# A hybrid decoder layer on one core: the first FFN matrix's operands behind the last load of w_out, the second gate product between the token groups, low halves one unit ahead

## The chip, the core and the metric

The kernel runs on one core of one Trainium2 chip. PE is its matrix engine (its weight loads are listed as PEld), DVE the vector engine, ACT the scalar engine, POOL a general engine, SP the engine that issues most DMAs. Each engine takes its instructions strictly in the order of the program and waits on semaphores for the others. The metric is the device time of one execution in microseconds.

## What is computed

One inference step of one decoder layer, for a prompt of 1024 tokens and for 8 samples of one token each, with d_model 1024 and d_ff 2816. All data is fp32. Cut to its core:

```python
def layer(x, c):
    sh, sc, gt = split(silu(c) @ w_ada_mix + b_ada_mix, 3)
    h = x * (1 + sc) + sh
    q, k, v, rq, rk, rv, rg = split(h @ w_in)
    att = window_attention(rope(q), rope(k), v, sinks)      # 8 heads of 64, window 128
    ret = silu(rg) * group_norm(retention(rope(rq), rope(rk), rv))  # 4 heads of 128, chunks of 128
    x = layer_norm(ALPHA * x + (1 + gt) * (concat(att, ret) @ w_out))
    sh, sc, gt = split(silu(c) @ w_ada_ffn + b_ada_ffn, 3)
    g, u = split((x * (1 + sc) + sh) @ w_up, 2)
    return layer_norm(ALPHA * x + (1 + gt) * ((silu(g) * u) @ w_down))
```

The samples use cached keys, values and retention states instead of earlier tokens, and the new keys, values and states are outputs too.

## The kernel before, in words

**Products.** An fp32 product is made from three reduced-precision ones. Every operand x is split into a high half (a cast, on ACT, line 269 for weights and 1347 for others) and a low half, x minus the high half (a subtraction on DVE, line 281 for weights, 1348 for others). `mm3` (line 213) then issues high×high, high×low and low×high (lines 215, 216, 217 of the profile). So no product on line 216 with a weight's low half (`wl`) can run before DVE has made it.

**Weight pages.** The input and output projections take their weights in units of one page (128 x 1024). `w_get` returns unit i and sets others on their way by `depth` = [loads, high halves, low halves] ahead of it. At first it is [2, 1, 0]. In the second half of the output projection it is set to [4, 4, 3].

**Stages.** After the start come the input projections of two halves of 512 tokens, then the output projection of half 0 and of half 1 (`out_proj`, line 1128). Each half runs over two column groups (cg) of 512 columns, four units of w_out each (kp), and four tiles of 128 tokens (t). The w_out units are the pages 46 to 53 for half 0 and 54 to 61 for half 1. All four tiles are computed per unit, except for the last column group of half 1, pages 58 to 61 (`by_tile`): there tile 0 goes through all units first, then tiles 1, 2 and 3, each followed by its own output and layer norm. The samples' share of the output projection (`poutz`) rides along in half 1. Then come layer norm 1 (`ln1_tile`, and `ln1_s` for the samples), the modulated, transposed FFN input of a token group of 512 tokens (`h2_group`: transposes into `h2p` on PE, `ht` on ACT, the differences `ts` and the halves `hb`, `hs`, `hc` on DVE and ACT), 22 up matrices and the down pass, and layer norm 2.

**The FFN.** Two by two blocks of a product are made with seven products instead of eight, so sums of blocks of the weights are needed besides the blocks. `up_prep(n)` releases all steps due up to n: the loads of a matrix (`wr`), its four sums on DVE (`sa`, `sb`, lines 1366 to 1369), and its halves `wa`, `wb`, `wc`, `wd`. For the first matrix, `out_proj` calls it between the last tiles (t == 1: loads, t == 2: sums and the first halves). `f_end` makes such sums from a finished pair of FFN tiles (`fsa`, `fsb`), and `wd_sums` from w_down (`wta`, `wtb`).

**The order of the work.** Main generators (projections, FFN) hand out costs in ns. The class `Merge` interleaves side generators with them: attention, retention, sample work, gate products, norms. A generator that yields "need" waits until that name is in `done`; other yields give the PE cost and how long to pause. A scheduler then orders the instructions of DVE, ACT and POOL by its own estimates, so what finally stands in a row on an engine is told by the built program, not by the code alone.

**Other parts that the change touches.** `ada_gate_a` and `ada_gate_b` make the gate of a sublayer: eight loads of 512 KB (`adr`), four blocks of products (`adab`, line 878), and two selections (`gsels`, line 902). Number 1 gates the mixer, number 2 the FFN. Both run before the output projection of half 0 or in it. `samp_ret` updates the samples' retention states with 32 DVE operations (line 994) from pages `st` and `vb`. `samp_sum` adds the four row groups in which PE leaves the samples' products. `ret_M` scales the retention output and splits it. In the last product of the down pass (`finish`) the first KM of its 11 units are computed for four tiles together, and the rest tile by tile in an order written by hand, each tile followed by its norm. A page pool of 46 pages and a pool of 8 PSUM banks hold everything.

## Time and profile before

| | us |
|---|---|
| median of 3 runs | 1256.14 |
| lowest, highest | 1255.63, 1257.42 |
| the profiled run | 1258.56 |
| its span | 1256.8 |

The mean granted clock of PE in the profiled run was 0.980. A row of the profile's timeline gives start, length, engine, line, operation, output and inputs by the program's names, shapes and, in brackets, how long the engine stood idle before and what released it. Records that follow one another closely are joined (x4), and the lengths of PE's matmuls overlap, since they are pipelined; from one start to the next is the pitch.

### The profile page before, as it was taken

To read this page: it belongs to the slowest core of one execution; us is meant where nothing else is said; L and a number is where in the kernel's file an instruction comes from. 1 tells how busy PE (TensorE), PEld (TensorE's weight loads), DVE (VectorE), ACT (ScalarE), POOL (GpSimd) and SP (SyncE) were. 2 spreads that over 40 slices of the span, in tenths; PEclk is the share of its full clock that TensorE was granted. 3 is DMA by queue.
4 is the path that set the end of the run, shared out by engine and by line. 5 is a ranking of instruction groups with operands and counts; after the bars stand their busy time and mean duration, and the time that the engine had idled before them with its cause. 6 is when DMAs were issued, how large, how long until landed. Compare 5 with 4: busy or idle time off the path is not lost.

```text
span 1256.8 us, 20184 instructions
## 1 busy us (share of the span) xinstructions
PE 1213.2 (97%) x7923; PEld 1023.8 (81%) x7923; DVE 875.0 (70%) x1749; ACT 469.6 (37%) x876; POOL 93.9 (7%) x130
## 2 busy tenths in 40 slices
PE   8999989999999999987999999999999999999996
PEld 5877756788877677677999999999999987888885
DVE  3456665787654687877767676667666769849697
ACT  2345543355543335545232322232223234434420
POOL 0000000001000002020110111011101110000011
PEclk8999999999999999997999999999999999999998
DMA  9732387242226432412443444344434499746631
GB/s 290 230 118 68 125 271 258 68 153 87 68 68 217 147 124 79 149 69 68 147 165 109 163 156 159 110 156 156 159 110 167 144 362 389 264 152 218 201 119 67
DMA packets 143999, 198.81 MB, mean 158 GB/s; under 512 B 8127, under 2 KB 85163, under 8 KB 143888
## 3 DMA queue, kind: packets, MB, share of 16 engines
q1 hardware_dynamic: 133376, 161.11, 39.6%
q0 software_dynamic: 10528, 36.42, 7.5%
q8 instruction: 62, 1.02, 0.3%
q14 instruction: 33, 0.27, 0.1%
HBM read 154.76 MB, written 43.77 MB: 158 GB/s over the span
## 4 chain that ended last, share of the span: by engine, by line
PE 54%; issue 29%; DVE 9%; POOL 4%; DMA 2%; ACT 1%; POOLq 0%; SPq 0%; DVEq 0%
PE pin L215 6%; PE pin L216 6%; PE pin L217 6%; PE dn L216 4%; PE dn L217 4%; PE dn L215 4%; PE up L215 2%; PE up L217 2%; PE up L216 2%; PE adab L878 2%; PE pout L215 1%; POOL fd L1486 1%; PE pv L671 1%; PE sps L628 1%; PE pout L216 1%
## 5 line engine op out<-in xcount | busy, mean ns | idle before, releaser
L215 PE MATMUL pin<-wh,hT 128*128 128x512 f32 (+1 forms) x320 | 129.6, 410 | 1.8 <-ACT qk L781 1.6
L216 PE MATMUL pin<-wl,hT 128*128 128x512 f32 (+1 forms) x320 | 124.8, 390 | 3.3 <-DVE wl L281 3.3
L217 PE MATMUL pin<-wh,hT 128*128 128x512 f32 (+1 forms) x320 | 124.3, 390 | 0.0
L215 PE MATMUL up<-hb,wa_h 128*128 128x256 f32 (+1 forms) x352 | 100.3, 286 | 6.9 <-ACT wa_h L1347 3.3
L216 PE MATMUL up<-hb,wa_h 128*128 128x256 f32 (+1 forms) x352 | 100.4, 285 | 0.4 <-DVE hb L1308 0.4
L217 PE MATMUL up<-hb,wa_l 128*128 128x256 f32 (+1 forms) x352 | 100.1, 285 | 0.2 <-DVE wa_l L1348 0.2
L215 PEld LDWEIGHTS pin<-wh,hT 128*128 128x128 f32 x320 | 61.1, 192 | 31.0 <-issue 13.9
L281 DVE TENSOR_TENSOR wl<-raw,wh 128x1024 fp32r<-128x1024 f32 (+1 forms) x62 | 73.1, 1183 | 7.3 <-ACT wh L269 3.6
L215 PEld LDWEIGHTS up<-hb,wa_h 128*128 128x128 f32 x352 | 67.3, 192 | 7.6 <-ACT wa_h L1347 3.5
L216 PEld LDWEIGHTS pin<-wl,hT 128*128 128x128 f32 x320 | 61.5, 192 | 14.4 <-DVE wl L281 3.4
L217 PEld LDWEIGHTS pin<-wh,hT 128*128 128x128 f32 x320 | 61.2, 191 | 14.0 <-issue 0.8
L1453 ACT ACTIVATE sg<-sg 128x256 f32<-128x256 f32 (+1 forms) x63 | 26.4, 420 | 115.3 <-DVE sg L1452 115.3
L216 PEld LDWEIGHTS up<-hb,wa_h 128*128 128x128 f32 x352 | 67.6, 192 | 0.6 <-DVE hb L1308 0.6
L217 PEld LDWEIGHTS up<-hb,wa_l 128*128 128x128 f32 x352 | 67.4, 192 | 0.4 <-DVE wa_l L1348 0.4
L269 ACT CAST wh<-raw 128x1024 fp32r<-128x1024 f32 (+1 forms) x62 | 62.9, 1020 | 6.8 <-DMA raw<-in_w_in 6.3
L1472 ACT COPY hTs<-sg 128x8 f32<-128x8 f32 x22 | 4.3, 198 | 138.9 <-DVE sg L1459 138.9
L1458 DVE TENSOR_TENSOR uc<-up,tp 128x256 f32<-128x256 f32 x66 | 28.2, 427 | 39.0 <-PE up L217 38.9
L1452 DVE TENSOR_TENSOR sg<-up,tp 128x256 f32<-128x256 f32 (+1 forms) x63 | 26.7, 423 | 38.2 <-PE up L217 38.2
L216 PE MATMUL pout<-wl,mh 128*128 128x512 f32 x128 | 50.8, 397 | 2.5 <-DVE wl L281 2.5
L215 PE MATMUL pout<-wh,mh 128*128 128x512 f32 x128 | 51.1, 408 | 0.0
L217 PE MATMUL pout<-wh,ml 128*128 128x512 f32 x128 | 51.0, 398 | 0.0
L215 PE MATMUL up<-hc,wc_h 128*128 128x256 f32 (+1 forms) x176 | 49.9, 284 | 0.0
(508 smaller groups left out, 3624.4 us busy)
## 6 DMA issues: line engine op xcount, KB each, us to landing
wr<-in_w_up SPq DMA_DIRECT2D x44, 512.0 KB, 5.2
raw<-in_w_in SPq DMA_DIRECT2D x38, 512.0 KB, 3.6
adr<-in_w_ada_ffn SPq DMA_DIRECT2D x24, 512.0 KB, 3.9
wd<-in_w_down SPq DMA_DIRECT2D x22, 512.0 KB, 5.2
dr<-fs SPq DMA_DIRECT2D x44, 256.0 KB, 2.8
dr<-ws SPq DMA_DIRECT2D x44, 256.0 KB, 3.7
fd<-sg POOLq DMA_DIRECT2D x33, 256.0 KB, 3.9
dr<-fd SPq DMA_DIRECT2D x33, 256.0 KB, 7.3
```

The costliest lines, as they stand in the source:

```text
L215: PE.matmul(ps, lhsT=ah, rhs=bh, start=start, stop=False, skip_group_check=onto)
L216: PE.matmul(ps, lhsT=ah, rhs=bl, start=False, stop=False, skip_group_check=onto)
L217: PE.matmul(ps, lhsT=al, rhs=bh, start=False, stop=stop, skip_group_check=onto)
L269: A.copy(out=h[:, 0:n], in_=src[:, 0:n])
L281: V.tensor_sub(out=l[:, 0:n], in0=src[:, 0:n], in1=f(h[:, 0:n]))
L628: PE.matmul(bk[:, i1 * 256:i1 * 256 + n], lhsT=qT[b][:, h * 128:(h + 1) * 128], rhs=kv[:, k0 + off:k0 + 256], start=s == 0, stop=s == 1)
L671: PE.matmul(bk[64 * par:64 * par + 64, 0:256].rearrange("p (a c) -> p a c", a=2), lhsT=v, rhs=pv[:, kt, par::2, :], start=kt == k0, stop=k ...
L878: PE.matmul(b[32 * q:32 * q + 32, :], lhsT=cT[:, k2 * 4 + q, :], rhs=rr[q // 2][:, (q % 2) * 512:(q % 2) * 512 + 512], start=k2 == 0, stop ...
L1452: V.tensor_tensor(out=dst, in0=ps, in1=add, op=ALU.add)
L1453: A.activation(out=dst, in_=dst, func=AF.Silu)
L1458: V.tensor_tensor(out=t, in0=ps, in1=add, op=ALU.add)
L1486: G.dma_start(out=two(d) if p == 4 else d, in_=ap)
```

## The change

It moves work and changes how far ahead operands are made; nothing is computed otherwise than before, but for the order of a few sums.

- The weight depth becomes [3, 2, 1] in half 0 of the output projection and [3, 3, 2] in half 1.
- The first up matrix is prepared by a side generator, `up_first`, that starts once the last unit of w_out has been asked to load ("wload"), in five steps, and it ends with a Silu activation of one column.
- The gate product 2 runs after the samples' norm ("xns") instead of in half 0, so between the two token groups of the FFN input.
- `ln1_s` needs only the samples' output ("outs") and not the whole half.
- `samp_ret` loads its states one step ahead and pauses 6000 ns after each step.
- `samp_sum` uses two adds on wider rows instead of three; `ret_M` does four multiplications and then four subtractions.
- In the down pass `f_end` is cut in two, the last sums come at units 2 and 4, the samples' z at 6, and the affine steps at the units in `ZAT`. KM becomes 3.

```diff
-KM = 4
+ZAT = [6, 8, 10, 12, 14, 16, 18, 20, 22, 24, 25, 26, 27, 28, 29, 30]
+KM = 3
...
     def samp_sum(dst, b, n):
-        A.copy(out=dst, in_=b[0:8, 0:n])
-        for g in range(1, 4):
-            V.tensor_tensor(out=dst, in0=dst, in1=b[32 * g:32 * g + 8, 0:n], op=ALU.add)
+        t = tmp512("ssum")
+        A.copy(out=t[0:40, 0:n], in_=b[0:40, 0:n])
+        V.tensor_tensor(out=t[0:40, 0:n], in0=t[0:40, 0:n], in1=b[64:104, 0:n], op=ALU.add)
+        V.tensor_tensor(out=dst, in0=t[0:8, 0:n], in1=t[32:40, 0:n], op=ALU.add)
...
-                A.mul(oh[:, a], src, g)
-                V.scalar_tensor_tensor(out=ol[:, a], in0=src, scalar=g, in1=f(oh[:, a]), op0=ALU.mult,
-                                       op1=ALU.subtract)
+                hs.append((oh[:, a], ol[:, a], b[:, h * 128:(h + 1) * 128], gnT[:, h:h + 1]))
+        for oh, ol, src, g in hs:
+            A.mul(oh, src, g)
+        for oh, ol, src, g in hs:
+            V.scalar_tensor_tensor(out=ol, in0=src, scalar=g, in1=f(oh), op0=ALU.mult, op1=ALU.subtract)
...
     def ada_gate_a(which):
+        if which == 2:
+            yield "need", "xns"
...
+        def st_load(i):
             t = page(f"st{i}")
...
+        st_load(0)
...
         yield 0, 4000, 3000
+        st_load(1)
...
-            yield 430, 0
+            vb.pop(i)
+            if i < 2:
+                st_load(i + 2)
+            yield 430, 6000
...
-        if half == 1:
-            depth[:] = [4, 4, 3]
+        depth[:] = [3, 2, 1] if half == 0 else [3, 3, 2]
...
+                if half == 1 and cg == 1 and kp == 0:
+                    done.add("wload")
...
                 out_samp(cg, psz)
+                done.add("outs")
                 for t in range(4):
-                    if t == 1:
-                        up_prep(-AHEAD[1])
-                    if t == 2:
-                        up_prep(-AHEAD[0])
...
+    def up_first():
+
+        yield "need", "wload"
+        up_prep(-AHEAD[1])
+        yield 0, 4000
+        for n in (-3, -1, 1, 3):
+            up_prep(n)
+            yield 0, 0, 2500
+        t = small("silu", [128, 1])
+        A.activation(out=t, in_=identr[:, 0:1].bitcast(F32), func=AF.Silu)
+
     def ln1_s():
-        yield "need", ("out", 1)
+        yield "need", "outs"
...
+        for p, ap in ((1, a11), (2, a12), (4, a22)):
+            d = drp.tile([128, 512], F32, name=f"fd{p}_{P}")
+            G.dma_start(out=two(d) if p == 4 else d, in_=ap)
+            FD[p, P] = d
+        yield
+        sa, sb = page(f"fsa{P}"), page(f"fsb{P}")
...
-        f_end(NP - 1)
-        wd_sums(NP - 1)
+        fe = f_end(NP - 1)
+        next(fe)
+        for e in range(2):
+            r = (2 * (NP - 1) + e) * 128
+            WD[1 + e, NP - 1] = I["w_down"][r:r + 128, 0:512]
...
                 if n == 2:
+                    next(fe, None)
+                if n == 4:
+                    wd_sums(NP - 1)
+                if n == 6:
                     samp_z()
-                if 5 <= n < 21:
-                    z_affine((n - 5) // 2, (n - 5) % 2)
-                elif n == 21:
+                if n in ZAT:
+                    z_affine(ZAT.index(n) // 2, ZAT.index(n) % 2)
+                elif n == 23:
...
-        M.add([ada_gate_a(1), ada_gate_a(2)])
+        M.add([ada_gate_a(1)])
...
-        M.add([ada_gate_b(1), ada_gate_b(2)])
+        M.add([ada_gate_b(1)])
         M.run(out_proj(0, False), R3)
         M.add([ln1_tile(t) for t in range(4)] + [h2_group(0)], 2)
-        M.add([ln1_tile(t) for t in range(4, 8)] + [ln1_s(), h2_group(1)], 2)
+        M.add([up_first()])
+        M.add([ada_gate_a(2), ada_gate_b(2)])
+        M.add([ln1_s()])
+        M.add([ln1_tile(t) for t in range(4, 8)] + [h2_group(1)], 2)
```

Three places of the built program show what this does to the engines' order. The number behind a name tells instances apart; lines after the change are about ten to twenty higher.

First DVE, in the last column group of half 1. `otmp` are outputs of the first column group; `wl58` and `wl59` are the low halves of the first two pages of the last column group. Before:

```order
L1117 TENSOR_TENSOR otmp_4979<-pout0_4672,gate1_4091 128x512
L1117 TENSOR_TENSOR otmp_4982<-pout1_4673,gate1_4091 128x512
L1117 TENSOR_TENSOR otmp_4985<-pout2_4674,gate1_4091 128x512
L281 TENSOR_TENSOR wl59_4865<-raw59_4756,wh59_4758 128x1024
L1305 TENSOR_TENSOR ts0_2_4878<-ht0_2_4837 128x512
L1308 TENSOR_TENSOR hb0_2_4876<-ht0_2_4837,hb0_2_4876 128x512
```

and now:

```order
L1128 TENSOR_TENSOR otmp_4926<-pout0_4629,gate1_4220 128x512
L1128 TENSOR_TENSOR otmp_4929<-pout1_4630,gate1_4220 128x512
L1128 TENSOR_TENSOR otmp_4932<-pout2_4631,gate1_4220 128x512
L282 TENSOR_TENSOR wl58_4812<-raw58_4703,wh58_4705 128x1024
L1325 TENSOR_TENSOR ts0_2_4825<-ht0_2_4784 128x512
L1328 TENSOR_TENSOR hb0_2_4823<-ht0_2_4784,hb0_2_4823 128x512
```

The same slot now makes page 58's low half, where page 59's stood. Some twenty rows further on (`lst` are statistics, `xrs` the samples' rows, `otz` and `ssum` their sums), before:

```order
L1217 BN_STATS lst_5141<-xr1_2_4935 128x6
L1118 SCALAR_TENSOR_TENSOR xr1_3_4937<-xr1_3_4937,otmp_4988 128x512
L1126 SCALAR_TENSOR_TENSOR xrs_4939<-xrs_4939,otz_4991 8x512
L281 TENSOR_TENSOR wl60_4945<-raw60_4861,wh60_4863 128x1024
L281 TENSOR_TENSOR wl61_5002<-raw61_4941,wh61_4943 128x1024
L408 TENSOR_TENSOR otz_5037<-otz_5037,poutz_5016 8x512 x3
L1124 TENSOR_TENSOR otz_5037<-otz_5037,gates_4068 8x512
```

and now:

```order
L1226 BN_STATS lst_5033<-xrs_4886 8x6
L1226 BN_STATS lst_5041<-xr1_0_4878 128x6
L282 TENSOR_TENSOR wl59_4892<-raw59_4808,wh59_4810 128x1024
L1226 BN_STATS lst_5099<-xr1_1_4880 128x6
L282 TENSOR_TENSOR wl60_4953<-raw60_4888,wh60_4890 128x1024
L409 TENSOR_TENSOR ssum_5018<-ssum_5018,poutz_4973 40x512
L282 TENSOR_TENSOR wl61_4965<-raw61_4949,wh61_4951 128x1024
```

Page 59's low half has moved here, ahead of pages 60 and 61, which stand where they stood. On PE the first product that needs it is in tile 0, behind products of page 58 in three tiles and a sample product of page 60:

```order
L216 MATMUL pout2_4947<-wh58_4705,mh1_0_3133 128x512
L217 MATMUL pout2_4947<-wl58_4812,mh1_0_3133 128x512
L218 MATMUL pout2_4947<-wh58_4705,ml1_0_3134 128x512
L216 MATMUL pout2_4947<-wh59_4810,mh1_1_3187 128x512
L1186 MATMUL poutz_4973<-raw60_4888,mixTs_73 32x512
L217 MATMUL pout0_4945<-wl59_4892,mh1_1_3187 128x512
L218 MATMUL pout0_4945<-wh59_4810,ml1_1_3188 128x512
L216 MATMUL pout0_4945<-wh59_4810,mh1_1_3187 128x512
```

Before, tile 0 went through both pages in one piece:

```order
L215 MATMUL pout0_4998<-wh58_4688,mh1_0_3121 128x512
L216 MATMUL pout0_4998<-wl58_4760,mh1_0_3121 128x512
L217 MATMUL pout0_4998<-wh58_4688,ml1_0_3122 128x512
L215 MATMUL pout0_4998<-wh59_4758,mh1_1_3256 128x512
L216 MATMUL pout0_4998<-wl59_4865,mh1_1_3256 128x512
L217 MATMUL pout0_4998<-wh59_4758,ml1_1_3257 128x512
L215 MATMUL pout0_4998<-wh59_4758,mh1_1_3256 128x512
L216 MATMUL pout0_4998<-wl59_4865,mh1_1_3256 128x512
```

Next PE around the transposes of the samples' rows (`h2ps`, from `xrs`). Before, they stood behind products of the first up matrix (`up`, with `wc0`):

```order
L217 MATMUL up_5259<-hs0_2h_4896,wc0_l_5208 128x256
L215 MATMUL up_5259<-hs0_3h_4922,wc0_h_5207 128x256
L216 MATMUL up_5259<-hs0_3l_4923,wc0_h_5207 128x256
L217 MATMUL up_5259<-hs0_3h_4922,wc0_l_5208 128x256
L1264 MATMUL h2ps_5272<-cst_66,xrs_4939 128x8 x8
L1292 MATMUL h2p_5285<-cst_66,xr1_0_4931 128x128
```

and now:

```order
L216 MATMUL pout2_4947<-wh61_4951,mh1_3_4236 128x512
L217 MATMUL pout2_4947<-wl61_4965,mh1_3_4236 128x512
L218 MATMUL pout2_4947<-wh61_4951,ml1_3_4237 128x512
L1284 MATMUL h2ps_5080<-cst_66,xrs_4886 128x8 x8
L216 MATMUL pout3_4948<-wh58_4705,mh1_0_3133 128x512
L217 MATMUL pout3_4948<-wl58_4812,mh1_0_3133 128x512
L218 MATMUL pout3_4948<-wh58_4705,ml1_0_3134 128x512
```

They have moved ahead of every product of the last tile (`pout3`).

Last DVE at the start of the down pass (`sg` and `uc` end the FFN's activation, `d1_1l` is the low half of the second down unit). Before:

```order
L1459 TENSOR_TENSOR sg21_10342<-sg21_10342,uc_10672 128x260
L1480 TENSOR_TENSOR fsb10_10678<-sg20_10243,sg21_10342 128x512
L1482 TENSOR_TENSOR fsa10_10677<-sg20_10243 128x512
L1481 TENSOR_TENSOR fsa10_10677<-fsb10_10678,sg20_10243 128x512
L1513 TENSOR_TENSOR wtb10_10698<-wd10_0_10475 128x512
L1483 TENSOR_TENSOR fsb10_10678<-sg21_10342,fsa10_10677 128x512
L1514 TENSOR_TENSOR wta10_10697<-wd10_1_10477,wd10_0_10475 128x512
L1515 TENSOR_TENSOR wta10_10697<-wd10_1_10477,wtb10_10698 128x512
L1516 TENSOR_TENSOR wtb10_10698<-wd10_1_10477,wta10_10697 128x512
L1348 TENSOR_TENSOR d1_1l_10729<-dr1_1_10482,d1_1h_10728 128x1024
L1348 TENSOR_TENSOR d1_2l_10733<-dr1_2_10485,d1_2h_10732 128x1024
```

and now:

```order
L1479 TENSOR_TENSOR sg21_10344<-sg21_10344,uc_10674 128x260
L1368 TENSOR_TENSOR d1_1l_10707<-dr1_1_10484,d1_1h_10706 128x1024
L1368 TENSOR_TENSOR d1_2l_10711<-dr1_2_10487,d1_2h_10710 128x1024
L1368 TENSOR_TENSOR d1_3l_10732<-dr1_3_10490,d1_3h_10731 128x1024
L1649 TENSOR_TENSOR z0_10726<-z0_10726,ln1_wb_10687 128x1024
L1649 TENSOR_TENSOR z0_10726<-z0_10726,ln1_bb_10690 128x1024
L1368 TENSOR_TENSOR d1_4l_10753<-dr1_4_10493,d1_4h_10752 128x1024
L1504 TENSOR_TENSOR fsb10_10771<-sg20_10245,sg21_10344 128x512
```

The eight sums (`fsa`, `fsb`, `wta`, `wtb`) that stood ahead of the low halves have moved behind them.

More of the change, by code (lines that the diff above doesn't have):

```diff
@@ L828, in ret_M @@
         half, tl = c // 4, c % 4
+        hs = []
         for j in range(2):
@@ L834, in ret_M @@
                 h = 2 * j + a
-                src, g = b[:, h * 128:(h + 1) * 128], gnT[:, h:h + 1]
-                A.mul(oh[:, a], src, g)
-                V.scalar_tensor_tensor(out=ol[:, a], in0=src, scalar=g, in1=f(oh[:, a]), op0=ALU.mult,
-                                       op1=ALU.subtract)
+                hs.append((oh[:, a], ol[:, a], b[:, h * 128:(h + 1) * 128], gnT[:, h:h + 1]))
[3 more added lines that the diff above has]
+            V.scalar_tensor_tensor(out=ol, in0=src, scalar=g, in1=f(oh), op0=ALU.mult, op1=ALU.subtract)
     def ret_chunk(c):
@@ L954, in samp_ret @@
         yield "need", ("zs", "rq")
-        state_pg = []
-        for i in range(4):
+        state_pg, vb = {}, {}
+        def st_load(i):
             t = page(f"st{i}")
@@ L959, in samp_ret @@
                          in_=I["state"][8 * i:8 * i + 8].rearrange("a d e -> d a e"))
-            state_pg.append(t)
+            state_pg[i] = t
+            t = page(f"vb{i}")
+            SP.dma_start(out=t[:, 0:1024], in_=vd[2 * i:2 * i + 2, :].rearrange("(o b) e -> o (b e)", o=1)
+                         .to_broadcast([128, 1024]))
+            vb[i] = t
+        st_load(0)
         rr = page("rrs")
@@ L963, in samp_ret @@
         ropefull(rr[0:8, 512:1024], zkvs[:, 0:512], C("src")[32:40], C("srs")[32:40], 8)
-        vb = []
-        for i in range(4):
-            t = page(f"vb{i}")
-            SP.dma_start(out=t[:, 0:1024], in_=vd[2 * i:2 * i + 2, :].rearrange("(o b) e -> o (b e)", o=1)
-                         .to_broadcast([128, 1024]))
-            vb.append(t)
         yield 0, 4000, 3000
+        st_load(1)
         b = bank("srt")
@@ L986, in samp_ret @@
         for i in range(4):
-            st = state_pg[i]
+            st = state_pg.pop(i)
             s4 = st[:, 0:1024].rearrange("p (b h e) -> p b h e", b=2, h=4)
@@ L1473, in f_end @@
                    in_=t[:, 512:NT].rearrange("p (b c) -> p b c", b=2)[:, :, 256:260])
-        sa, sb = page(f"fsa{P}"), page(f"fsb{P}")
         def two(ap):
             return ap.rearrange("p (b c) -> p b c", b=2)
+        for p, ap in ((1, a11), (2, a12), (4, a22)):
[4 more added lines that the diff above has]
+        sa, sb = page(f"fsa{P}"), page(f"fsb{P}")
         s2, s3, s1, s4 = sa[:, 0:512], sa[:, 512:1024], sb[:, 0:512], sb[:, 512:1024]
@@ L1483, in f_end @@
         V.tensor_sub(out=s4, in0=a12, in1=s2)
-        for p, ap in ((1, a11), (2, a12), (4, a22)):
-            d = drp.tile([128, 512], F32, name=f"fd{p}_{P}")
-            G.dma_start(out=two(d) if p == 4 else d, in_=ap)
-            FD[p, P] = d
         for p2, t in (((6, 7), sa), ((5, 3), sb)):
@@ L1530, in emit @@
         n0 = 14 * (P + 1)
-        side.setdefault(n0, []).append((f_end, P))
+        side.setdefault(n0, []).append((lambda P: list(f_end(P)), P))
         side.setdefault(n0 + 1, []).append((wd_load, P))
```

## The prediction

> **What bounds the kernel now.** I read the busy shares first, then the windows, then what the engines wait for.
>
> ```profile
> PE 1213.2 (97%) x7923; PEld 1023.8 (81%) x7923; DVE 875.0 (70%) x1749; ACT 469.6 (37%) x876; POOL 93.9 (7%) x130
> span 1256.8 us, 20184 instructions
> ```
>
> PE is busy 97% of the span, so an edit pays only by giving PE less to do or by taking away a wait of PE. All sums go against this profiled run (1258.56 us with what lies around the span). The median of the runs shown is 1256.14, so I take 2.4 off at the end. Where PE loses time, the windows say (start:end, length, busy of PE, weight load, DVE, ACT, POOL, granted clock, DMA share, GB/s):
>
> ```profile
> 180.00:190.00 10.00, 7.69 (x43) 5.34 (x44) 10.00 (x39) 0.84 (x2) 0.00 (x0) 0.83 0.79 259
> 530.00:540.00 10.00, 8.77 (x38) 6.16 (x37) 9.80 (x15) 1.52 (x2) 0.00 (x0) 1.00 0.00 0
> 544.20:589.70 45.50, 32.94 (x215) 29.90 (x213) 34.98 (x79) 27.70 (x41) 5.49 (x9) 0.85 0.29 94
> ```
>
> The largest hole is the transition from the output projection to the FFN. There the reader should follow one clock. Let H be the start of the first h2 transposes of token group 0, 499.79, which the change leaves where they are in PE's order; T3 the end of the last output tile, 544.18 = H+44.4; the first use of the second up matrix's low half, 589.68 = H+89.9, closes the stretch.
>
> ```profile
> 499.79 0.60 PE L1292 MATMUL h2p<-cst,xr 128*128 128x128 f32 x4
> 516.00 1.06 PE L1174 MATMUL poutz<-raw,mixTs 128*32 128x512 f32 x8
> 533.88 0.50 PE L216 MATMUL pout<-wl,mh 128*128 128x512 f32 x1 [1.23 <-DVE wl L281]
> 544.18 0.28 PE L215 MATMUL up<-hb,wa_h 128*128 128x256 f32 x1
> 550.55 0.38 PE L215 MATMUL up<-hb,wa_h 128*128 128x256 f32 x1 [3.12 <-ACT tp L1434]
> 587.40 0.58 PE L215 MATMUL up<-hb,wa_h 128*128 128x256 f32 x1 [3.26 <-ACT wa_h L1347]
> 589.68 0.58 PE L217 MATMUL up<-hb,wa_l 128*128 128x256 f32 x1 [0.15 <-DVE wa_l L1348]
> ```
>
> Before T3 PE waits only 1.23; behind it, 32.94 us of PE work take 45.5.
>
> **The change, part by part. 1, the low halves in the transition (a loss).** DVE is full here, so its order is a timetable.
>
> ```profile
> 516.05 1.22 DVE L281 TENSOR_TENSOR wl<-raw,wh 128x1024 fp32r<-128x1024 f32 x1
> 517.18 0.68 DVE L1305 TENSOR_TENSOR ts<-ht 128x512 f32<-128x512 f32 x1
> 517.79 0.69 DVE L1308 TENSOR_TENSOR hb<-ht,hb 128x512 fp32r<-128x512 f32 x1
> ...
> 532.62 2.34 DVE L281 TENSOR_TENSOR wl<-raw,wh 128x1024 fp32r<-128x1024 f32 x2
> ```
>
> The row at 516.05 is the low half of w_out page 59. The 24 operations behind it run without a gap to 532.62 (15.4 us), and a 512-wide one takes 0.6 (517.18 to 517.79). PE did not notice, since it had pages 58 and 59 for all four tiles. With the depth [3, 3, 2] that slot makes page 58 instead, and page 59 comes behind 23 operations. They are the same but for one add and one statistic fewer (−1.3), and two low halves of hs_2 and hs_3 that now stand right behind their own ts, with nothing between to cover the ACT cast:
>
> ```profile
> 508.22 1.23 DVE L1348 TENSOR_TENSOR hs_0l<-ts,hs_0h 128x1024 fp32r<-128x1024 f32 x1 [1.11 <-ACT hs_0h L1347]
> ```
>
> That is +2×1.1. So page 59's low half is ready at 17.5 (516.05+1.2 less H) + 15.4 − 1.3 + 2.2 + 1.2 = H+35.0. PE leaves w57 at the same H+16.2 (516.00), waits for page 58 to 17.5, and has 22 products of w58 and high halves and 5 sample products: 22×0.235 + 0.7 = 5.9, H+23.4. The pitch 0.235 is from these rows, two apart:
>
> ```profile
> 543.48 0.39 PE L215 MATMUL pout<-wh,mh 128*128 128x512 f32 x1
> ...
> 543.94 0.40 PE L217 MATMUL pout<-wh,ml 128*128 128x512 f32 x1
> ```
>
> **New wait: 11.6 us** (10 to 12), with every later matrix product queued behind it. Next, the sample rows' transposes (h2ps) now stand in front of the whole of tile 3. They need xrs, normalised by ACT after DVE has done what stands ahead of its statistics: five low halves (pages 60 and 61, and wa, wb, wc of the first up matrix) at 1.15, sixteen operations 512 wide (sample sums, block sums of the up matrix, outputs and statistics of two tiles) at 0.6, and five small ones of 0.6 together. That is 16 us, with small waits 17 to 18, and ACT's normalisation, 1.24 as in the row at 552.98 below, makes H+53.3 to 54. PE arrives at 35.0 + 51×0.235 + 0.5 = H+47.5. **Second new wait: about 6** (4 to 7). Then 0.7 for h2ps, 24×0.235 for tile 3 and 1 for a gate block give H+61.3; the clock adds 0 to 3, I take 1.2. So T3 is at H+62.5 instead of H+44.4, **18 lost**.
>
> The clock: PE waited 3.12 before 550.55 and 3.26 before 587.40, and the granted clock over 544 to 590 was 0.85, against 1.00 from 530 to 540, where its one wait was 1.23. The Trainium skill, "TensorE: Matmul & The Clock Gate", Part 1 (The HAM clock gate), says that an idle window of about 3.4 us halves the clock until PE has been busy for about as long. The trace agrees in size, though its waits were each a little shorter. By that rule both new waits are followed by half speed, some 1.7 each, 2.2 more than I take.
>
> **2, behind T3 (a gain).** Before, the first ht of the second group came at 561.03, T3+16.8, because up_prep's work stood between.
>
> ```profile
> 552.98 1.24 ACT L1238 ACTIVATE xr<-xr,lrs 128x1024 f32<-128x1024 f32 x1 [1.53 <-DVE lrs L1236]
> 554.24 1.28 ACT L1450 ACT_TABLE_LOAD   x1
> ...
> 561.03 1.45 ACT L1293 ACTIVATE ht<-h2p,B,A 128x512 f32<-128x512 f32 x2 [2.34 <-PE h2p L1292]
> ```
>
> Now the first up matrix is ready before T3, so only the last tile's norm is left: two halves of add and statistic, the small steps and ACT's 1.24 make about 4.3, and the transposes T3+5.2: **11.6 gained**. From there the same chain runs to the low half, 589.68 − 561.03 = 28.7, plus two gate operations on DVE at 0.7: T3+35.3. Together H+97.8 against H+89.9: **+7.9** for parts 1 and 2 (+3 to +16, the top from the third rival). The table load stays (below).
>
> **3, the second gate product leaves the first half.** There PE has no hole.
>
> ```profile
> 400.00:450.00 50.00, 50.00 (x265) 34.65 (x264) 33.00 (x88) 17.58 (x39) 2.61 (x3) 0.97 0.39 138
> 417.38 1.06 PE L878 MATMUL adab<-adr,cT 128*32 128x512 f32 x8
> 418.26 1.02 PE L902 MATMUL gsels<-adg,cst 128*9 128x512 f32 x2
> ```
>
> Four blocks at 0.9 (417.38 to 418.26) and two selections at about the same are 5.4 to 6.3: **−5.9**. One block goes ahead of T3 (counted above), the rest behind it, where PE has idle time. Their eight loads wait for pages that the first up matrix frees, the first pair for the last of its low halves, at about H+48, and land so much later:
>
> ```profile
> adr<-in_w_ada_ffn SPq DMA_DIRECT2D x24, 512.0 KB, 3.9
> ```
>
> That is H+52, some 3 us before PE comes to the first block, so I cost their wait at nothing; two or three us more of landing would show as a wait of PE in front of tile 3.
>
> **4, the first half's own waits.** Page 51 and the retention transposes cost PE little now.
>
> ```profile
> 456.56 0.51 PE L216 MATMUL pout<-wl,mh 128*128 128x512 f32 x1 [1.23 <-DVE wl L281]
> 481.21 0.66 PE L827 MATMUL rmt<-cst,sm 128*128 128x128 f32 x4 [1.35 <-DVE sm L753]
> ```
>
> The sample attention now stands in this half, with one low half ahead. By the same rows I expect four or five waits of 0.4 to 2, in all 4.5 instead of 3.0: **+1.5** (−2 to +3). The regrouped gn multiplies (four on ACT, then four on DVE) hide under the products between two chunks; if they do not, a chunk's second half is late by one 128-wide step, under 0.4.
>
> **5, sample retention.**
>
> ```profile
> 182.18 4.28 DVE L994 SCALAR_TENSOR_TENSOR st<-vb,kss,st 128x128 f32<-128x128 f32 x16
> 182.31 0.50 PE L216 MATMUL pin<-wl,hT 128*128 128x512 f32 x1 [3.31 <-DVE wl L281]
> ```
>
> State updates stood in DVE's queue in blocks of 16 and delayed a low half by 3.31; the clock in that window was 0.83, 1.7 more. Spread over 6 us steps they no longer pile up, but other banks are then waited for, which no row here shows; I take one wait like that at 456.56 above, with a little clock, 1.5: **−3.5** (−6 to +2).
>
> **6, the start of the down pass.**
>
> ```profile
> 1027.40 0.69 DVE L1480 TENSOR_TENSOR fsb<-sg,sg 128x512 f32<-128x512 f32 x1
> ...
> 1032.34 1.22 DVE L1348 TENSOR_TENSOR d_1l<-dr,d_1h 128x1024 fp32r<-128x1024 f32 x1
> 1033.61 0.50 PE L216 MATMUL dn<-d_1l,d_1h 128*128 128x512 f32 x1 [1.60 <-DVE d_1l L1348]
> ```
>
> Eight sums of 0.6 stood ahead of the second low half. Now they come later and PE has a stock. The waits here list as 1.6, 1.1, 0.4 and 0.3: **−3.0** (−0.5 to −3.4).
>
> **7, edits beside other work.** The two adds instead of three in the sample sums save DVE 0.6 each; only those of the transition stand on the path, and they are counted there. The affine steps, spread over more units of the down pass, and the later sums lie beside products on an engine that is 70% busy; if the cover is gone, a unit waits for one of them, 1.3 at most (an affine step is 1024 wide, as the low half of 1.22). I take 0.
>
> **8, tail and start.** With KM = 3 a tile of the hand-written tail has eight units instead of seven, 24×0.235 = 5.6 us of PE instead of 4.9, so DVE's norms fall less behind PE and end nearer its last product (1246.3): **−0.7** (0 to −1.6) of this lag.
>
> ```profile
> 1245.92 0.39 PE L217 MATMUL dn<-d_10h,d_10l 128*128 128x512 f32 x1
> 1247.90 0.68 DVE L1657 TENSOR_TENSOR zt<-dn,gate 128x512 f32<-128x512 f32 x1
> ```
>
> The Silu warm-up depends on nothing, so the order has it at ACT's very start, with two more table loads of 1.28 (row 554.24) there, and other functions run in between; the load in the transition stays. Cost at the start 0 to 2.6, hidden beside the first loads: **+0.5**. The Trainium skill, "ScalarE: Activation LUTs", section What ACT_TABLE_LOAD costs, gives 2.66 us for a switch, drain included; by that figure it would be up to 5.3, but no row here shows the drain.
>
> **Sum:** 7.9 − 5.9 + 1.5 − 3.5 − 3.0 − 0.7 + 0.5 = −3.2; 1258.56 − 3.2 = 1255.4 as a profiled run, **1253 on the median's scale**.
>
> **The rivals.** *The low halves do not decide* (the two new waits stay away because DVE gets to page 59 earlier than I count). T3 is then H+45.4 and the close H+80.7, −9.2 instead of +7.9: total −20.3, **1236**. Against it: DVE's stretch had no idle time to give back (9.80 of 10). *PE becomes the bound behind T3* (slower). Window 544.20 shows 32.94 us of PE work at a clock of 0.85, about 26 at full speed; with three gate blocks and two selections some 31. The chain leaves it 35.3. If the clock stays at 0.85 (7 us more) and half of the 12.5 us idle returns because PE meets these blocks in its order before the transposes of the last chunks, it takes T3+44: +16.6, total +5.5, **1262**. It decides once half clock and waits there exceed 4 us. *The warm-up does not do what it says*: in the sum already. *The retention and down-pass gains are not collected* (their waits return at the next page): +6.5, **1259.5**.
>
> **How the numbers follow.** Forecast 0.45, first rival 0.17, second 0.25, last 0.13. A measurement of this kernel can tell about 0.2%, 2.5 us: faster is under 1253.6, slower above 1258.7. The forecast, with its terms' spread of about ±4, splits 0.25 faster, 0.16 same, 0.04 slower; the first rival is all faster; the second 0.02, 0.05, 0.18; the last 0.01, 0.05, 0.07. Together 0.45, 0.26, 0.29. The range 1239 to 1263 leaves out most of the first rival and a little above; the forecast's own is 1249 to 1257.
>
> **What would show it.** Right: a PE wait of 10 to 12 us for wl some 24 us after the h2p transposes, one of 4 to 7 for xrs before the last tile, T3 near H+62, the first ht of group 1 five us behind it, no L994 block ahead of wl, no wait for d_1l. Wrong: T3 near H+45; a wait for adr; PE without idle time between T3 and the second up matrix; a wait of more than 3 us in the first half.

## The result, and the profile after

The changed kernel is slower: 1267.07 us median (1265.95 to 1269.29, 4 runs) against 1256.78 (1255.63 to 1258.2, 4 runs) of the kernel before; the ratio is 1.0086, 95% interval 1.0068 to 1.0103. The prediction of 1253, with a range that ended at 1263, was wrong in sign. Its profiled run took 1265.95 us, 7.4 more than the one of before, which lay 1.8 above the median of 1256.78, while that of the change lies 1.1 below its own; the medians differ by 10.3.

The page's first lines of the changed kernel (span, then busy time of each engine):

```profile
span 1264.2 us, 20177 instructions
PE 1216.0 (96%) x7923; PEld 1019.0 (81%) x7923; DVE 868.4 (69%) x1741; ACT 469.3 (37%) x879; POOL 92.6 (7%) x130
```

PE does the same 7923 products. Of the 7.4 us by which the profiled span grows, 4.6 are more idle time of PE and 2.8 more busy time. Where they lie, the windows of the changed kernel tell (columns as in the prediction; the second is H to T3, the third T3 to the second up matrix):

```profile
180.00:190.00 10.00, 10.00 (x64) 6.14 (x64) 6.41 (x27) 3.13 (x6) 0.00 (x0) 1.00 0.73 231
493.00:560.10 67.10, 50.75 (x228) 33.86 (x227) 46.21 (x81) 27.18 (x35) 6.33 (x11) 0.87 0.40 132
560.10:598.30 38.20, 33.93 (x235) 26.00 (x233) 26.48 (x58) 22.53 (x36) 1.65 (x3) 0.97 0.45 154
```

The hole at 182 is gone. H to T3 takes 67.1 us instead of 44.4, and for 16.4 of these PE stands idle. PE's timeline of the changed kernel shows the two waits that the prediction named, at nearly the sizes it gave (11.6 and about 6):

```profile
493.02 0.60 PE L1312 MATMUL h2p<-cst,xr 128*128 128x128 f32 x4
...
529.35 0.80 PE L217 MATMUL pout<-wl,mh 128*128 128x512 f32 x1 [10.20 <-DVE wl L282]
529.94 0.63 PE L218 MATMUL pout<-wh,ml 128*128 128x512 f32 x1
530.37 0.63 PE L216 MATMUL pout<-wh,mh 128*128 128x512 f32 x1
...
551.02 1.02 PE L1284 MATMUL h2ps<-cst,xrs 8*128 8x8 f32 x8 [6.15 <-ACT xrs L1247]
...
560.11 0.28 PE L216 MATMUL up<-hb,wa_h 128*128 128x256 f32 x1
...
598.27 0.55 PE L218 MATMUL up<-hb,wa_l 128*128 128x256 f32 x1
```

The last row is the first use of the second up matrix's low half, which closes the stretch at H+105.2. Behind the first wait the pitch is 0.43 (529.94 to 530.37) instead of 0.23, so PE runs at half speed. DVE's timeline of the changed kernel shows who is late, and one wait that the prediction did not have:

```profile
509.70 1.21 DVE L282 TENSOR_TENSOR wl<-raw,wh 128x1024 fp32r<-128x1024 f32 x1
...
528.09 1.20 DVE L282 TENSOR_TENSOR wl<-raw,wh 128x1024 fp32r<-128x1024 f32 x1
...
534.80 0.69 DVE L409 TENSOR_TENSOR ssum<-ssum,poutz 40x512 f32<-40x512 f32 x1 [3.78 <-ACT ssum L408]
...
541.81 1.22 DVE L1368 TENSOR_TENSOR wa_l<-wr,wa_h 128x1024 fp32r<-128x1024 f32 x1
542.95 1.22 DVE L1368 TENSOR_TENSOR wb_l<-sa,wb_h 128x1024 fp32r<-128x1024 f32 x1
544.08 1.22 DVE L1368 TENSOR_TENSOR wc_l<-sb,wc_h 128x1024 fp32r<-128x1024 f32 x1
```

Page 58's low half comes at 509.70, page 59's at 528.09. The samples' sum then waits 3.78 us, since the sample products on PE are queued behind products that wait for page 59.

The waits of PE at the start of the down pass, changed kernel (us in total, times, longest):

```profile
PE dn L217 <- DVE d_0l L1368: 1.0, 1, 1.0
PE dn L217 <- DVE d_8l L1368: 1.0, 1, 1.0
PE dn L216 <- ACT d_1h L1367: 0.3, 1, 0.3
```

Together 2.3 instead of 3.4: d_1l is no longer waited for, but d_8l is.

### The profile page after: what moved, and what is told of

It reads as the page before. It is cut to its first block, busy times and chain, and to the rows that moved or that the text cites. A ratio compares the mean times of both kernels' runs of the same rounds, so it can differ in the third digit from the quotient of the medians.

```text
span 1264.2 us, 20177 instructions
## 1 busy us (share of the span) xinstructions
PE 1216.0 (96%) x7923; PEld 1019.0 (81%) x7923; DVE 868.4 (69%) x1741; ACT 469.3 (37%) x879; POOL 92.6 (7%) x130
## 4 chain that ended last, share of the span: by engine, by line
PE 41%; issue 29%; DVE 7%; POOL 4%; DMA 1%; ACT 1%; POOLq 0%; DVEq 0%; ACTq 0%
PE dn L217 4%; PE dn L216 4%; PE dn L218 4%; PE pin L216 3%; PE pin L218 3%; PE pin L217 3%; PE up L216 2%; PE up L217 2%; PE up L218 2%; PE pout L217 2%; PE pout L218 2%; PE pout L216 2%; POOL fd L1499 1%; POOL fs L1510 1%; POOL ws L1539 1%
## 5 line engine op out<-in xcount | busy, mean ns | idle before, releaser
L216 PEld LDWEIGHTS pin<-wh,hT 128*128 128x128 f32 x320 | 60.0, 188 | 25.8 <-issue 11.6
L218 PEld LDWEIGHTS pin<-wh,hT 128*128 128x128 f32 x320 | 60.3, 188 | 15.1 <-issue 2.5
L217 PEld LDWEIGHTS pin<-wl,hT 128*128 128x128 f32 x320 | 60.3, 189 | 10.6 <-DVE wl L282 1.1
```

What stands on the lines that cost most here:

```text
L216: PE.matmul(ps, lhsT=ah, rhs=bh, start=start, stop=False, skip_group_check=onto)
L217: PE.matmul(ps, lhsT=ah, rhs=bl, start=False, stop=False, skip_group_check=onto)
L218: PE.matmul(ps, lhsT=al, rhs=bh, start=False, stop=stop, skip_group_check=onto)
```

## The experiments

All times are medians; a ratio is against the runs of the kernel before on the same chip. To compare stages I read four rows in the one profiled run of each kernel: H (the first h2p row), T3 (the first product of the up matrices), M3 (the first product of the third up matrix, by which all work moved here is done), and S (the first matrix product of half 1's output projection, the 193rd of 384).

S is needed because H does not stand at the same place of PE's order in every kernel: 239 of the 384 products are ahead of it before, 237 in the change, but 228 in b_depth and a_noret and 248 in f1, and a product takes some 0.23 us. What stands ahead of S is the same but for the parts that an edit moves. Between the change and before H serves as well.

| kernel | us | ratio (95%) | H | H to T3 | H to M3 | S | S to M3 |
|---|---|---|---|---|---|---|---|
| before | 1256.78 | 1 | 499.8 | 44.4 | 111.0 | 488.9 | 121.9 |
| the change | 1267.07 | 1.0086 (1.0068–1.0103) | 493.0 | 67.1 | 126.7 | 482.5 | 137.2 |
| e1_depth | 1263.72 | 1.0071 (1.0049–1.0093) | 493.4 | 62.5 | 122.3 | 481.6 | 134.1 |
| e2_h2ps | 1262.61 | 1.0058 (1.0036–1.0081) | 496.7 | 54.7 | 122.5 | 486.2 | 133.0 |
| e3_gate | 1267.06 | 1.0096 (1.0076–1.0115) | 496.9 | 66.9 | 123.9 | 487.5 | 133.2 |
| e4_prep | 1260.97 | 1.0046 (1.0030–1.0062) | 492.1 | 59.2 | 122.4 | 481.6 | 132.9 |
| e12 | 1258.57 | 1.0026 (1.0011–1.0041) | 495.2 | 48.5 | 118.3 | 483.4 | 130.2 |
| x1_fill | 1265.60 | 1.0073 (1.0053–1.0093) | 493.2 | 66.0 | 126.2 | 482.7 | 136.7 |
| f1 | 1261.75 | 1.0052 (1.0035–1.0069) | 495.9 | 42.1 | 118.9 | 482.9 | 131.9 |
| b_depth | 1261.70 | 1.0047 (1.0030–1.0065) | 493.3 | 55.3 | 118.8 | 485.0 | 127.1 |
| b_ret | 1263.68 | 1.0057 (1.0039–1.0075) | 501.8 | 48.2 | 112.4 | 490.4 | 123.8 |
| b_gain | 1260.56 | 1.0028 (1.0018–1.0039) | 502.2 | 48.2 | 112.6 | 490.8 | 124.0 |
| b_down | 1253.16 | 0.9987 (0.9972–1.0002) | 495.7 | 44.4 | 110.0 | 484.8 | 120.9 |
| f2 | 1256.81 | 1.0018 (1.0004–1.0032) | 497.5 | 41.7 | 111.4 | 485.1 | 123.7 |
| a_noret | 1265.25 | 1.0059 (1.0040–1.0077) | 492.3 | 66.5 | 126.8 | 484.0 | 135.2 |
| e1234 | 1258.07 | 1.0012 (0.9996–1.0028) | 501.2 | 45.4 | 109.6 | 488.8 | 122.0 |
| e1234_noret | 1250.25 | 0.9939 (0.9920–0.9959) | 492.5 | 45.7 | 109.8 | 480.3 | 122.0 |

S and M3 in PE's timeline of the kernel before, then of the changed kernel:

```profile
488.89 0.39 PE L215 MATMUL pout<-wh,mh 128*128 128x512 f32 x1
...
610.74 0.28 PE L215 MATMUL up<-hb,wa_h 128*128 128x256 f32 x1
```

```profile
482.52 0.39 PE L216 MATMUL pout<-wh,mh 128*128 128x512 f32 x1
...
619.76 0.28 PE L216 MATMUL up<-hb,wa_h 128*128 128x256 f32 x1
```

The same instructions do not always take the same time: b_down, b_depth and f2 have the program of before up to S and reach it at 484.8 to 485.1, the profiled run of before at 488.9. PE was busy 475.5 us up to there in that run instead of 470.3 to 470.6, at a granted clock of 0.98 instead of 0.99. From S to M3, b_down (120.9) and before (121.9), the same program there too, differ by 1.0.

**e1_depth: the depth of half 1 back.**

```diff
-        depth[:] = [3, 2, 1] if half == 0 else [3, 3, 2]
+        depth[:] = [3, 2, 1] if half == 0 else [4, 4, 3]
```

> The change with only the depth of half 1 set back to [4, 4, 3], so that page 59's low half is made where it was before. Theory A (two waits in a row: DVE's queue sets when xrs is ready, and xrs stands in front of the last tile): the 10.2 us wait for wl goes, but PE then waits longer for xrs, 10 to 12 us instead of 6.1, and runs at half clock behind it; the time falls by only 2 to 4 us, to 1263 to 1265. Rival B (the low half alone carries the loss, with the half clock behind it): the time falls by 12 to 15 us, to 1252 to 1255, and the wait for xrs does not grow.

Theory A's time, 1263.72. The wait for wl became one for page 60, and the wait for xrs grew. PE's timeline of e1_depth:

```profile
529.11 0.80 PE L217 MATMUL pout<-wl,mh 128*128 128x512 f32 x1 [6.75 <-DVE wl L282]
546.84 1.02 PE L1284 MATMUL h2ps<-cst,xrs 8*128 8x8 f32 x8 [7.77 <-ACT xrs L1247]
```

14.5 us of waiting instead of 16.4: PE waits for DVE's queue as a whole, and whichever page stands in it is only the place where that shows. The wait for xrs is shorter than the 10 to 12 expected, because the wait for page 60 had not been expected. S to M3 is 3.1 shorter.

**e2_h2ps: the samples' norm behind the half again.**

```diff
     def ln1_s():
-        yield "need", "outs"
+        yield "need", ("out", 1)
```

> The change with only the samples' norm waiting for the whole half again, as before; their transposes, and the gate product 2 which waits for them, then stand behind the last tile. Theory A: the wait of 6.1 us for xrs goes with its half clock (about 2 us), the 10.2 us wait for wl stays: T3 is 7 to 9 us earlier, of which the longer chain behind T3 takes back some 2; the time falls by 5 to 7 us, to 1260 to 1262. Rival B (the low half alone): falls by at most 2 us, 1265 to 1267. Rival C (the gate blocks in the stretch carry the loss): since they move behind the group's transposes, it falls by 3 to 4 us with the wait for xrs not mattering.

1262.61, just above theory A's 1260 to 1262. T3 moved from 67.1 to 54.7, more than the expected 7 to 9, but M3 only from 126.7 to 122.5: the last part of the gate product, which waits for the samples' norm, slid behind the second matrix's start and is paid there. Rival B (at most 2 us) is out.

**e12: both.** 

> Both: depth [4, 4, 3] in half 1 and the samples' norm behind the last tile. Theory A: neither wait is left, T3 lies some 45 to 48 us behind the first transposes instead of 67, and the early operands of the first up matrix now pay: 15 to 19 us less than the change, 1248 to 1252, so faster than the kernel before by 5 to 9. Rival B: the same as with the depth alone (within 2 us). Rival C (gate blocks): still 4 us or more over 1252.

A miss: 1258.57, where theory A said 1248 to 1252. Counted from S, T3 is 5.0 behind that of before (60.3 for 55.3) and M3 8.3. A wait of 3.7 us for a low half of w_out is left ahead of T3, and one of 3.8 for DVE behind it. So the two waits were not the whole loss.

**e3_gate: the gate product 2 back in half 0.**

```diff
     def ada_gate_a(which):
-        if which == 2:
-            yield "need", "xns"
...
-        M.add([ada_gate_a(1)])
+        M.add([ada_gate_a(1), ada_gate_a(2)])
...
-        M.add([ada_gate_b(1)])
+        M.add([ada_gate_b(1), ada_gate_b(2)])
...
-        M.add([ada_gate_a(2), ada_gate_b(2)])
```

> The change with only the gate product 2 back in the first half's projection. Theory A: the first half gets about 6 us longer, the stretch behind T3 3 to 5 us shorter (a gate block and its copy on ACT no longer stand in the chain of group 1), one block less before T3: within 2 us of the change, 1265 to 1269. Rival C (the gate blocks carry the loss in the transition): 8 us or more under the change.

As theory A said: 1267.06, no difference. S is 5.0 later, S to M3 4.0 shorter. What the move takes out of the first half it pays back in the transition. The chain there, ACT's timeline of the changed kernel:

```profile
565.56 1.45 ACT L1313 ACTIVATE ht<-h2p,B,A 128x512 f32<-128x512 f32 x2 [0.42 <-PE h2p L1312]
...
570.93 1.28 ACT L1470 ACT_TABLE_LOAD   x1
...
584.75 0.59 ACT L885 COPY adg<-adab 127x512 f32<-127x512 f32 x1 [3.19 <-PE adab L882]
585.24 0.41 ACT L1336 CAST hc<-ht 128x260 fp32r<-128x260 f32 x1
```

The copy of a gate block waits 3.19 us for PE, and the cast hc is queued behind it. DVE waits for that cast, as its timeline shows:

```profile
585.68 0.43 DVE L1337 TENSOR_TENSOR hc<-ht,hc 128x260 fp32r<-128x260 f32 x1 [2.84 <-ACT hc L1336]
```

**x1_fill: does the half clock cost the time?** 44 extra products keep PE busy where it stood for page 59; they compute nothing that is used.

```diff
+                    if by_tile and kp == 1 and kk == 0:
+                        fb = bank("fill")
+                        for _ in range(44):
+                            PE.matmul(fb, lhsT=MH[half, 0][:, 0:128], rhs=ws[0][0][:, 0:512], start=True, stop=True)
```

> The change, with 44 extra products of page 58 into an unused bank issued by PE ahead of page 59's products (10.3 us at full clock), so that PE works on instead of standing idle; the order of all other instructions is the change's. Theory A (after the 10.2 us wait PE ran some 10 us at half clock, and this delays the sample sums that DVE waits 3.8 us for): the products behind page 59's low half start at the same time but run at a pitch of 0.235 instead of 0.43, xrs is ready 2 to 3 us earlier, T3 3 to 5 us earlier: 1262 to 1265. Rival (DVE alone sets the time and the clock costs nothing): 1266 to 1268, although PE does 10 us more work.

1265.60 lies between theory A (1262 to 1265) and the rival (1266 to 1268); the stages decide. PE's timeline of x1_fill:

```profile
512.64 10.20 PE L1177 MATMUL fill<-wh,mh 128*128 128x512 f32 x43
...
529.59 0.50 PE L217 MATMUL pout<-wl,mh 128*128 128x512 f32 x1 [1.10 <-DVE wl L282]
529.93 0.39 PE L218 MATMUL pout<-wh,ml 128*128 128x512 f32 x1
530.16 0.39 PE L216 MATMUL pout<-wh,mh 128*128 128x512 f32 x1
...
549.13 1.02 PE L1288 MATMUL h2ps<-cst,xrs 8*128 8x8 f32 x8 [6.31 <-ACT xrs L1251]
...
550.67 0.63 PE L217 MATMUL pout<-wl,mh 128*128 128x512 f32 x1
551.10 0.63 PE L218 MATMUL pout<-wh,ml 128*128 128x512 f32 x1
```

The products behind page 59 run at full speed (0.23), and the wait for xrs ends 1.9 us earlier (549.13 for 551.02), as the mechanism says. DVE's wait for the sample products falls from 3.78 us to 1.65, as its timeline of x1_fill shows:

```profile
532.91 0.69 DVE L409 TENSOR_TENSOR ssum<-ssum,poutz 40x512 f32<-40x512 f32 x1 [1.65 <-ACT ssum L408]
```

From page 59's first product to the sample rows' transposes it is 19.5 us instead of 21.7, so half speed behind the first wait costs 2.1. But the wait for xrs is as long as in the change, with half speed behind it (0.43) that lasts longer here (granted clock 0.70 from the transposes to T3, 0.79 in the change): T3 is only 1.1 earlier, and M3 0.5. (The half clock that is taken away lasted about 5 us and not the 10 of the expectation, as the last section shows.) So half speed behind the first wait costs 2.1 at the transposes and 0.5 at M3, little of the 15 us that are lost there. The half clock behind the second wait has no run of its own.

**e4_prep: the first up matrix's preparation back between the last tiles** (the Silu of one column goes with it).

```diff
                 for t in range(4):
+                    if t == 1:
+                        up_prep(-AHEAD[1])
+                    if t == 2:
+                        up_prep(-AHEAD[0])
...
-        M.add([up_first()])
```

> The change with only the first up matrix's preparation put back between the last tiles. Theory A' (DVE's queue alone sets when xrs is ready; the clock does not): 6.4 us of DVE work (four sums, three low halves and wd) leave the queue ahead of xrs, so the wait for xrs goes and T3 comes 6 to 8 us earlier, while the 10.2 us wait for wl stays; the sums and low halves then fall behind T3, where they take most of it back: 1262 to 1266. Rival E (the wait for xrs comes from the samples' own sums and stays): T3 within 2 us of the change, and the time above 1267.

H to T3 is 59.2, 7.9 less than in the change, and no wait for xrs is left; the waits of PE in e4_prep from 440 to 600:

```profile
PE pout L217 <- DVE wl L282: 10.8, 2, 10.2
PE up L216 <- ACT wa_h L1371: 2.8, 1, 2.8
```

The early operands made xrs late, since they stood ahead of it in DVE's queue. M3 keeps 4.3 of the 7.9, and at 1260.97 the time fell a little further than expected.

**f1: e2 with the depth [4, 4, 4].** 

> The change with the samples' norm behind the last tile and the depth [4, 4, 4] in half 1, so that pages 59 and 60 both are made early. Theory A': no PE wait for wl over 1 us is left (3.7 in the run with [4, 4, 3], with two half-clock windows behind it), T3 is 4 to 6 us earlier than there; as the chain of group 1 starts no earlier than DVE lets it, half of that stays: 1254 to 1257. Rival (any T3 gain is given back behind it): 1258 to 1259.

A miss, and the rival's 1258 to 1259 too: 1261.75. T3 is as early as before (55.1 behind S for 55.3), yet M3 is 10.0 later than before and 1.7 later than in e12. PE's timeline of f1 shows where the gain went:

```profile
553.41 0.58 PE L216 MATMUL up<-hs_0h,wb_h 128*128 128x256 f32 x1 [5.13 <-DVE tp L1457]
```

An earlier T3 only meets a DVE that is not ready.

**b_depth: the depth alone, on the kernel before** ([4, 4, 3] to [3, 3, 2]). 

> The kernel before, with only the depth of half 1 changed from [4, 4, 3] to [3, 3, 2]. Theory A: page 59's low half slides behind some 25 DVE operations here too, PE waits about 10 us for it and then runs at half clock, T3 is 11 to 14 us later, and some of it is caught up behind T3 where DVE had a backlog of 12 us: 1262 to 1268. Rival D (the loss comes from the early operands of the up matrix that push into DVE's queue, and the depth does no harm alone): 1256 to 1258.

1261.70, just under theory A's range, and far from rival D. The waits of PE in b_depth from 440 to 600:

```profile
PE pout L216 <- DVE wl L281: 8.7, 2, 7.4
```

S to M3 is 5.2 longer than before, near the 5.9 that the ratio gives. (The 7.8 from H to M3 counts more work, since H stands eleven products earlier here.) So one low half less in stock costs this kernel 0.5% by itself.

**b_ret, b_gain, b_down: the parts outside the transition, on the kernel before.** b_ret has the sample retention's edit alone, b_down the end of the FFN, ZAT and KM, b_gain both.

```diff
...
-            yield 430, 0
+            vb.pop(i)
+            if i < 2:
+                st_load(i + 2)
+            yield 430, 6000
```

> The kernel before with only the sample retention's loads and pauses changed. As the prediction priced it (the 3.31 us wait for wl at 182 gone with its clock, 1.5 given back to banks): 3.5 under the kernel before, 1252 to 1253. Rival (the wait returns elsewhere, since the same 32 operations stay in DVE's queue): within 1 us of the kernel before.

> The kernel before with only the parts of the change that lie outside the transition: the sample retention's loads and pauses, the end of the FFN and the start of the down pass, KM = 3. By the traces so far these gain 1.4 to 3.5 before the output projection, 1.3 at the start of the down pass, 1.0 in the tail: 1250 to 1253. Rival (the sample retention only moves its waits): 1254 to 1256.

> The kernel before with only the down-pass part (end of the FFN, start of the down pass, KM = 3). As measured in the change's trace: 1.3 at the start of the pass and 1.0 in the tail: 1254 to 1256. As the prediction priced it: 3.7, 1252 to 1253.5.

The sample retention costs 0.57% instead of gaining 3.5 us: both theories missed. S stands at 490.4, against 484.8 in b_down, where the program up to S is that of before. b_gain carries the same loss (490.8). b_down is 1.7 faster by the median, with an interval that just includes no change.

**f2: b_down with the depth [4, 4, 4].** 

> The kernel before with the down-pass part of the change (end of the FFN, start of the down pass, KM = 3) and the depth [4, 4, 4] in half 1. The waits for d_1l (1.6) and wl (1.2) go, the tail ends 1 us nearer: 2 to 4 us under the kernel before, 1252 to 1255. Rival (each of them is hidden or moved): within 1 us of it.

1256.81, no gain, as in f1: it is 3.7 slower than b_down, from which only the depth differs, and S to M3 is 2.8 longer. T3 comes 1.3 earlier, M3 later. So a low half more in stock does not pay here either.

**e1234, a_noret, e1234_noret: undoing all of it.** e1234 undoes e1 to e4 together; a_noret undoes the sample retention in the change; e1234_noret does both.

> The change with all four parts of the transition undone: depth [4, 4, 3] in half 1, the samples' norm behind the half, the first up matrix's preparation between the last tiles, the gate product 2 in the first half. Theory F (the four parts make up the whole loss of the transition): from the first transposes to the second up matrix 97 to 101 us, as before, instead of 114, and the time is that of the kernel before plus the sample retention's cost: 1256 to 1262. Rival (other parts, such as the samples' sums, lengthen the transition too): that stretch over 103 us, the time over 1262.

> The change with only the sample retention's loads and pauses undone. Theory G (its operations, spread out, delay the work queued behind them on PE in the first half, as in the run with it alone): 3 to 6 us under the change, 1261 to 1264. Rival (the prediction's price: it gains 3.5 and the loss in the run alone came from another order of work in the first half): 1268 to 1271.

> The change with the four parts of the transition and the sample retention undone; what is left are the first half's depth [3, 2, 1], the samples' sums, the retention output's order, and the down pass with KM = 3. Theory F and G: 1 to 4 us under the kernel before, 1252 to 1255. Rival: the first half's depth costs something too: 1256 to 1260.

e1234 settles the transition: S to M3 is 122.0, that of the kernel before (121.9), and nothing else in the change lengthens it. The four single steps shortened it by 3.1, 4.2, 4.0 and 4.3, in sum 15.6; together they shorten it by 15.2, and the change had lengthened it by 15.3. (The 97 to 101 and 114 of the expectation belong to no marks of the table; from H to the second up matrix it is 87.6 before, 102.7 in the change and 86.5 in e1234.) But the time is still 1258.07, because S is at 488.8. a_noret gains only 1.8 by the medians, less than theory G's 3 to 6, and its interval overlaps the change's. With the transition undone the same edit is worth 7.8 (1258.07 to 1250.25). **e1234_noret is faster than both kernels**: 0.9939, interval 0.9920 to 0.9959, and more than was expected.

Where the sample retention's price shows, the groups of `adab` products ahead of H tell, in e1234 and then in e1234_noret (busy time, mean ns):

```profile
L882 PE MATMUL adab<-adr,cT 128*32 128x512 f32 x128 | 25.4, 605 | 0.0
```

```profile
L882 PE MATMUL adab<-adr,cT 128*32 128x512 f32 x128 | 19.1, 604 | 0.0
```

The same 128 records take 6.3 us longer. One block in each, from their timelines, e1234 first:

```profile
411.50 1.04 PE L882 MATMUL adab<-adr,cT 128*32 128x512 f32 x2
412.67 1.05 PE L882 MATMUL adab<-adr,cT 128*32 128x512 f32 x2
414.31 1.05 PE L882 MATMUL adab<-adr,cT 128*32 128x512 f32 x4
```

```profile
410.16 1.07 PE L882 MATMUL adab<-adr,cT 128*32 128x512 f32 x8
```

A block's eight records take 1.07 us in one piece, and a piece of a broken one takes 1.04 to 1.05, whether it has two records or four. (Two of e1234's pieces, of two records each, take 0.6.) Counted over the whole run, the blocks stand in 25 pieces in e1234 and in 18 in e1234_noret. With the spread retention steps the blocks are cut up more in PE's order, and these 6.3 us are most of the 8.5 between the two S. In b_ret it is 22 pieces for the 19 of b_down and 23.3 us for 20.1, only 3.2 of the 5.6 between their S. In the change itself it is 19 pieces ahead of H for the 14 of a_noret, yet S does not come later (482.5 for 484.0): the granted clock up to S was 0.97 in a_noret and 0.98 in the change, and why is open. No run keeps the blocks whole with the steps spread, so that the price is measured, but this cause of it is read from the traces only.

## Why the prediction was wrong, point by point

- **Part 1, the two new waits: right in place and size, T3 too early by 4.6.** 10.2 for 11.6, 6.15 for 6; page 59 ready at H+36.3 for H+35.0. The second size came out by luck: PE reached the transposes at H+51.8 instead of H+47.5, and xrs came as much later, at H+58.0 instead of H+53.3 to 54. T3 came at H+67.1 instead of H+62.5. The failed term is the clock, taken at 1.2. From page 59's first product to the transposes it is 21.7, counted as 17 to 18 plus 1.24: DVE waited 3.78 there for the sample products (row 534.80), which stand behind page 59's on PE, and x1_fill shows that 2.1 of it are half speed. From the transposes to T3 it is 9.1, counted as 7.3 without the clock, at a granted clock of 0.79. That makes some 3.9 for the clock. Page 59 being 1.3 later makes most of the rest.
- **Part 2, behind T3: too large by 3.** The first ht came at T3+5.4 (row 565.56 in ACT's timeline) for T3+5.2, so the early operands did what was said of them. The close came at T3+38.2 for T3+35.3. What failed is "the rest behind it, where PE has idle time" in part 3: a gate block held ACT and with it the chain of group 1 (584.75), and with the gate product back the close stood at T3+35.2, the predicted figure. This is close to the second rival's mechanism, gate blocks that hold up the last chunks, at a third of its price (2.9 of 8.7).
- **Parts 1 to 3 together** gave 7.9 for H to the close; it was 105.2 − 89.9 = 15.3. The sum's largest term was half of what was measured. The four steps of it add up (e1 to e4), so there is no single edit that carries the loss.
- **Part 3, the first half's gain: −5.9 predicted, −5.0 measured** (S of e3_gate against the change).
- **Part 4, the first half's own waits: +1.5 predicted.** With transition and retention undone, S is at 480.3 against 484.8 in b_down, so these edits gain some 4.5 instead. PE stands idle 12.2 us up to S in place of 14.5. That comparison is of two profiled runs.
- **Part 5, sample retention: wrong in sign.** The hole at 182 went, as said (PE busy 10.00 of 10), but the edit costs 5.6 us up to S in b_ret and 8.5 in e1234, and the 1.5 for "other banks are then waited for" was not what took the hole's place: in the traces the blocks of `adab` products stand in more pieces on PE, +6.3 us ahead of H in e1234. The price was set by the nearest wait and not by asking what the moved steps push apart on PE.
- **Part 6, down pass: −3.0 predicted, −1.1 measured** in waits; d_8l replaced d_1l. **Part 8, tail: −0.7 predicted, −1.0 measured**: the last product starts 9.9 before the span's end (1264.2 − 1254.34) instead of 10.9 (1256.8 − 1245.92), as these rows of the changed kernel and the spans show.

```profile
1254.11 0.39 PE L217 MATMUL dn<-d_10l,d_10h 128*128 128x512 f32 x1
1254.34 0.39 PE L218 MATMUL dn<-d_10h,d_10l 128*128 128x512 f32 x1
```

- **The warm-up** does not do what it says, as forecast: the table load stays in the transition, at 570.93 on ACT (row above).
- **The reference.** The sum started from a profiled run of before that reached S 3.8 to 4.1 later than three other runs of the same instructions. So of the 6.4 us that the change seems to gain up to S, some 2.5 are its own. With 15.3 lost from S to M3 and 1.6 gained behind it, that makes 11.2, near the 10.3 of the medians.

## What to carry to other kernels

Where one engine is full, its program order is a timetable: count operations between two needs, and a stock of one item less, or work pulled forward, shows up as a wait that this count foretells (11.6 counted, 10.2 measured). A gain at one point of such a chain (an earlier T3, a full clock) is given back in part or whole, until the next thing that the full engine has to deliver is earlier too; measure it at a mark behind all the moved work, and from a mark that the edits do not move. And an edit that only spreads small steps can cost more than the wait it removes (a wait of 3.31 us went, 5.6 to 8.5 us came); what it cuts apart on the bound engine is the first place to look.

## What the runs showed of the hardware that was not expected

- Products that each fill 32 rows of the output took 1.07 us together when a block's eight records followed one another, and nearly every piece of two or four records took 1.04 to 1.05 us when other products came between (rows 411.50 to 414.31 and 410.16). The same 128 records were busy 25.4 us in 25 pieces and 19.1 in 18.
- The clock halves during a wait and stays so behind it. In the windows of the changed kernel below (columns as above), the first is the wait for page 59, the next two are the products behind it, and the last shows the half clock by itself, 0.50. At 0.74 the clock is half for 5.3 of the 10.2 us of waiting, and at 0.56 for another 4.9 of busy products. The Trainium skill's page "TensorE: Matmul & The Clock Gate", Part 1 (The HAM clock gate), asks for at least one busy window of about 3.4 us before the clock is full again. Here 4.9 us of products passed first.

```profile
519.15:529.35 10.20, 0.00 (x1) 0.01 (x1) 9.26 (x14) 2.47 (x3) 0.00 (x0) 0.74 0.00 0
529.40:535.00 5.60, 5.60 (x16) 2.77 (x17) 1.82 (x3) 0.81 (x2) 0.00 (x0) 0.56 0.00 0
535.00:539.60 4.60, 4.60 (x21) 3.75 (x20) 4.50 (x7) 0.73 (x1) 0.00 (x0) 1.00 0.00 0
524.20:534.20 10.00, 4.85 (x13) 2.15 (x13) 6.71 (x9) 0.50 (x2) 0.00 (x0) 0.50 0.00 0
```
